# Long convolution of a hybrid encoder layer: the second DFT step on two columns at a time, with half-array matmuls and one ring of three PSUM banks

## The chip, the cores and the metric

One core of a Trainium2 chip runs the whole program. The metric is the device time of one execution in microseconds (us).

## The reference

One encoder layer is applied to two requests (256 and 2048 rows of 1024 values, all float32). An input projection gives a Hyena group (512 channels) and an attention group; both are normalised, projected and followed by a gated MLP. What this case touches is the Hyena group's long convolution, an FFT product over twice the sequence, done twice (order 2) for each request:

```python
def long_conv(z, kf, skip):
    L = z.shape[1]
    zf = z.astype(jnp.float32)
    y = jnp.fft.irfft(jnp.fft.rfft(zf, n=2 * L, axis=1) * kf[None], n=2 * L, axis=1)[:, :L]
    return (y + skip.astype(jnp.float32) * zf).astype(z.dtype)

def hyena_mixer(u, short_w, short_b, w1, b1, sin_freq, w2, b2, w3, decay, skip):
    L = u.shape[1]
    u = dwconv3(u, short_w, short_b)
    v, x1, x2 = jnp.split(u, 3, axis=-1)
    kf = hyena_filters(L, w1, b1, sin_freq, w2, b2, w3, decay)
    z = x1 * long_conv(v, kf[:, 0], skip[0])
    z = x2 * long_conv(z, kf[:, 1], skip[1])
    return z
```

The attention is a dilated sliding-window attention over 8 heads; its queries, keys and values come out of the same input projection.

## The kernel before

**The convolution in four steps.** A DFT of 2L points is split in two factors, 128 and `n2c` = 2L/128 (4 for the short request, 32 for the long one). `hyena_first` does the first factor (two matmuls `hs1`, lines 692 and 693) and stores the result in DRAM (`d_hA`). `hyena_second` works on `n2c` columns g, each a tile of 128 rows (64 real parts, 64 imaginary) by 512 channels: a float32 matmul with the table `htab` of g gives the filter's spectrum (`hs2k`, line 723), VectorE scales it (`hK`, line 725), a second matmul gives the signal's spectrum (`hs2z`, line 727), VectorE makes the four partial products of the complex product in four instructions on 64 partitions each (lines 731 to 734), GpSimd adds them (line 735), and one column later a matmul takes the product back (`hs3`, line 741; its tile is called `hs` in the trace), ScalarE copies it to `hbe` (line 744), and a DMA stores two columns in `d_hB`. The last step, in `hyena`, loads `hD` from `d_hB`, does two matmuls that use 64 of the array's columns each (`hs4`, line 778), multiplies with the gate (line 779) and either feeds `hyena_first` again (order 0) or stores to `d_hy` (order 1). There are 36 columns in each order, 72 in all, so 36 pairs of columns.

**PSUM and rings.** The pool `h_ps` has three banks: two in turn for `hs2k` and `hs2z` (tag `hps`), one for `hs1`, `hs3` and `hs4` (tag `hpt`). SBUF tiles of two columns come from the ring `hr` (4 buffers), `hk` has one buffer.

**What runs beside it.** `weave` runs generators in turn: at each step it takes the stream whose count of steps is smallest against its rate. In the first part the convolution (rate 135) runs beside the second half of the input projection, query, key and value columns (matmuls `pj`, transposes `pjt`); in the second part (rate 90) beside the attention (rate 440; scores `aS`, transposes `aT`, values `aOp`). Each `yield` is a step. Before, `hyena_second` has a yield after each column's products and one after each column's `hs3`: four for a pair of columns; the whole convolution has 216 steps. From the order in which the program is written, the framework's scheduler makes an order of instructions for each engine; each engine then runs its own in that order. When both streams have ended, the output projection (`om`, with transposes `ot`) goes through 9 chunks of 256 rows; the first chunk is the short request, and every later chunk needs rows of `d_hy` that the long request's last `hs4` steps write.

The choice of the next stream is this:

```python
            x = min(live, key=lambda y: (y[2] + 0.5) / y[1])
            x[2] += 1
```

Of the kernel before, what the change touches and what calls it, by code (L numbers as in the profile page):

```python
# [21 lines left out]
P = 128  # L22
# [26 lines left out]
def _dft(L):  # L49
# [34 lines left out]
    ti = np.transpose(t, (0, 2, 1))  # L84
# [105 lines left out]
class Hybrid:  # L190
# [488 lines left out]
    def hyena_first(self, wp, psp, r, An, n, z):  # L679
# [3 lines left out]
        for k in range(2):  # L683
# [6 lines left out]
            for h in range(2):  # L690
                ps = psp.tile([P, C], F32, tag="hpt", name="hs1", bufs=1)
# [6 lines left out]
    def hyena_second(self, wp, psp, r, o, A, B):  # L698
# [10 lines left out]
        be = None  # L709
        for g in range(n2c + 1):  # L710
            cur = None
            if g < n2c:
                i = g % 2
                if i == 0:
                    gs = slice(g, g + 2)
                    tab = wp.tile([P, 2, 2, P], F32, tag="htab", name="htab", bufs=2)
                    nc.sync.dma_start(out=tab, in_=self.a[f"tab_{r}"][:, gs])
                    xz = self.ring(wp, "hx")
                    nc.sync.dma_start(out=xz, in_=Ag[:, gs])
                    xk = wp.tile([P, 2, C], F32, tag="hk", name="hk", bufs=1)  # L720
                    nc.sync.dma_start(out=xk, in_=Kg[:, gs])
# [16 lines left out]
            if prev is not None:  # L738
# [3 lines left out]
                if g2 % 2 == 0:  # L742
                    be = self.ring(wp, "hbe")
                nc.scalar.copy(be[:, g2 % 2], ps)
                if g2 % 2 == 1:
                    nc.sync.dma_start(out=Bg[:, g2 - 1:g2 + 1], in_=be)
# [939 lines left out]
```

## Time and profile before

| | us |
|---|---|
| median of 3 executions | 3562.38 (3561.86 to 3563.61) |
| the profiled execution | 3565.03 |
| its span in the trace | 3562.9 |
| TensorE busy | 3303.1 (93%) |
| VectorE busy | 2465.5 (69%) |
| ScalarE busy | 1561.9 (44%) |
| GpSimd busy | 1255.2 (35%) |
| granted TensorE clock, mean | 0.957 |

The profiled execution took 2.1 us more than its span in the trace shows, and 2.7 us more than the median. In the trace a matmul's end is modelled and matmuls overlap, so TensorE's throughput is read from the distance between the starts of successive instructions, not from their durations. A float32 matmul of the program stands in the trace as two instructions.

### The profile page before, as it was taken

The numbers are of one execution on the slowest core, as the hardware profiler recorded it, in microseconds if no ns is written. First come the engines' busy times: TensorE is split into PE (matmuls) and PEld (weight loads), VectorE is DVE, ScalarE is ACT, GpSimd is POOL, SyncE is SP. The second block draws the span as 40 slices with busy tenths as digits, with TensorE's granted clock in tenths as the row PEclk, the third lists the DMA queues.
The fourth block names the chain that finished last, engine by engine and source line by source line (L and its number), as shares of the span: only waits on it lengthen the run. The fifth ranks groups of instructions, "written<-read, shape, count | busy, mean of one in ns | idle before, by whom it ended". The sixth has DMA issues, their size and how long they took to land.

```text
span 3562.9 us, 56859 instructions
## 1 busy us (share of the span) xinstructions
PE 3303.1 (93%) x20926; PEld 3020.3 (85%) x20926; DVE 2465.5 (69%) x4254; ACT 1561.9 (44%) x2926; POOL 1255.2 (35%) x946
## 2 busy tenths in 40 slices
PE   7989899999899999996588799999899999899998
PEld 4978798889677788773388799999899999899998
DVE  7898877764576564686388666766776666567657
ACT  4577753323345565541255433333433334344433
POOL 1487751124222231222144433333634333223222
PEclk9999999999989999997699899999999999999999
DMA  6453567676756585656666632444544224466655
GB/s 240 134 179 122 154 186 240 225 223 199 202 173 194 149 235 157 187 176 195 212 188 199 198 108 106 153 154 151 218 147 150 95 94 147 155 205 217 221 179 181
DMA packets 408334, 628.02 MB, mean 176 GB/s; under 512 B 28431, under 2 KB 231439, under 8 KB 402135
## 3 DMA queue, kind: packets, MB, share of 16 engines
q1 hardware_dynamic: 354896, 593.13, 51.2%
q10 hardware_dynamic: 52072, 28.40, 2.7%
q8 instruction: 166, 2.72, 0.3%
q0 software_dynamic: 1088, 2.85, 0.2%
q14 instruction: 112, 0.92, 0.1%
HBM read 419.03 MB, written 205.25 MB: 175 GB/s over the span
## 4 chain that ended last, share of the span: by engine, by line
PE 58%; DVE 7%; DMA 7%; issue 2%; ACT 2%; SPq 1%; POOL 1%; ACTq 0%; DVEq 0%; POOLq 0%
PE w L210 8%; PE w L208 8%; PE w L209 8%; PE fd L210 4%; PE fd L209 4%; PE fd L208 4%; PE aOp L938 4%; PE aS L906 2%; PE aS L907 2%; PE aT L922 2%; PE hs2k L723 1%; PE hs2z L727 1%; PE hs L741 1%; PE pj L209 1%; PE pj L208 1%
## 5 line engine op out<-in xcount | busy, mean ns | idle before, releaser
L208 PE MATMUL w<-hh,whi 128*128 128x288 f32 (+1 forms) x2464 | 735.4, 299 | 16.3 <-ACT whi L1345 9.9
L210 PE MATMUL w<-hh,wlo 128*128 128x290 f32 (+1 forms) x2464 | 732.2, 298 | 10.7 <-POOL wlo L203 7.0
L209 PE MATMUL w<-hl,whi 128*128 128x288 f32 (+1 forms) x2464 | 735.2, 299 | 5.2 <-DVE hl L203 5.1
L208 PEld LDWEIGHTS w<-hh,whi 128*128 128x128 f32 x2464 | 470.3, 191 | 18.2 <-ACT whi L1345 10.1
L210 PEld LDWEIGHTS w<-hh,wlo 128*128 128x128 f32 x2464 | 469.4, 191 | 12.7 <-POOL wlo L203 8.0
L209 PEld LDWEIGHTS w<-hl,whi 128*128 128x128 f32 x2464 | 472.0, 192 | 6.7 <-DVE hl L203 6.6
L208 PE MATMUL pj<-hThi,wihi 128*128 128x386 f32 (+1 forms) x1152 | 402.5, 350 | 6.6 <-ACT u L629 4.1
L209 PE MATMUL pj<-hTlo,wihi 128*128 128x386 f32 (+1 forms) x1152 | 400.9, 348 | 7.8 <-DVE hTlo L203 7.8
L210 PE MATMUL pj<-hThi,wilo 128*128 128x386 f32 (+1 forms) x1152 | 397.8, 345 | 0.0
L208 PE MATMUL fd<-hh,dwh 128*128 128x288 f32 x1210 | 359.9, 297 | 12.6 <-ACT dwh L1551 12.6
L210 PE MATMUL fd<-hh,dwl 128*128 128x288 f32 x1210 | 358.8, 297 | 0.0
L209 PE MATMUL fd<-hl,dwh 128*128 128x288 f32 x1210 | 357.5, 295 | 0.0
L735 POOL TENSOR_TENSOR ht<-ht,ht 128x512 f32<-128x512 f32 x72 | 99.0, 1376 | 432.3 <-DVE ht L734 364.1
L208 PEld LDWEIGHTS fd<-hh,dwh 128*128 128x128 f32 x1210 | 229.8, 190 | 13.3 <-ACT dwh L1551 12.9
L209 PEld LDWEIGHTS pj<-hTlo,wihi 128*128 128x128 f32 x1152 | 221.8, 193 | 20.7 <-DVE hTlo L203 9.7
L938 PEld LDWEIGHTS aOp<-aV,aPT 128*128 128x128 f32 (+1 forms) x1408 | 193.9, 196 | 52.5 <-issue 20.3
L208 PEld LDWEIGHTS pj<-hThi,wihi 128*128 128x128 f32 x1152 | 221.1, 192 | 17.7 <-ACT u L629 4.4
L210 PEld LDWEIGHTS pj<-hThi,wilo 128*128 128x128 f32 x1152 | 220.9, 192 | 12.2 <-issue 8.0
L209 PEld LDWEIGHTS fd<-hl,dwh 128*128 128x128 f32 x1210 | 229.3, 190 | 0.4
L210 PEld LDWEIGHTS fd<-hh,dwl 128*128 128x128 f32 x1210 | 227.6, 188 | 0.1
L203 POOL TENSOR_TENSOR wlo<-ws,whi 128x512 fp32r<-128x512 f32 x88 | 133.4, 1516 | 235.9 <-ACT whi L1345 235.9
L910 DVE CUSTOM_DVE_ANT_0 aP<-aS,aB 128x256 f32<-128x256 f32 (+2 forms) x432 | 136.2, 355 | 115.6 <-PE aS L907 43.4
(297 smaller groups left out, 7977.3 us busy)
## 6 DMA issues: line engine op xcount, KB each, us to landing
hl<-d_G SPq DMA_DIRECT2D x154, 288.0 KB, 5.3
dwl<-d_S SPq DMA_DIRECT2D x59, 704.0 KB, 4.1
wiraw<-in_w_in SPq DMA_DIRECT2D x72, 512.0 KB, 4.6
d_G<-cv SPq DMA_DIRECT2D x42, 576.0 KB, 3.0
wraw<-in_w_gate SPq DMA_DIRECT2D x22, 1024.0 KB, 4.8
wraw<-in_w_up SPq DMA_DIRECT2D x22, 1024.0 KB, 5.6
adat<-in_ada_t SPq DMA_DIRECT2D x36, 512.0 KB, 4.6
d_fA<-fae SPq DMA_DIRECT2D x72, 256.0 KB, 3.1
```

The source lines that it names most:

```text
L203: eng.tensor_tensor(out=lo, in0=x, in1=hi.bitcast(F32), op=ALU.subtract)
L208: mm(out, wh, xh, start=first, stop=False, skip_group_check=more)
L209: mm(out, wh, xl, start=False, stop=False, skip_group_check=more)
L210: mm(out, wl, xh, start=False, stop=last, skip_group_check=more)
L723: nc.tensor.matmul(ps, tab[:, i, 0], xk[:, i], start=True, stop=True)
L727: nc.tensor.matmul(ps, tab[:, i, 0], xz[:, i], start=True, stop=True)
L735: nc.gpsimd.tensor_tensor(out=t1, in0=t1, in1=t2, op=ALU.add)
L906: nc.tensor.matmul(ps[:, hh, :N], qa, rhs, start=True, stop=False)
L907: nc.tensor.matmul(ps[:, hh, :N], qb, rhs, start=False, stop=True)
L910: nc.vector.tensor_tensor_reduce(out=sb[:, hh, :n], in0=ps[:, hh, v0:v0 + n], in1=bias[:, hh, b0:b0 + n], scale=1.0, scalar=3e38, op0=ALU. ...
L922: nc.tensor.transpose(pt[:cn, hh, c], sb[:, hh, c0:c0 + cn], self.ident)
L938: nc.tensor.matmul(po[:, i, hs], pe[:cn, hh, c], vt[:cn, x["v"] + c * x["vs"], hs], start=(c == 0), stop=(c == len(ch) - 1))
```

## The change

The table of the inverse step is laid out anew on the host, so that its rows of the real parts of two columns stand together, and those of the imaginary parts.

`hyena_second` now takes a pair of columns in each round. A helper `forward` fills one PSUM bank with the real parts of both columns (j = 0) or with the imaginary parts of both (j = 1), by two matmuls that use all 128 rows and 64 columns of the array each; one writes partitions 0 to 63, the other 64 to 127. So real and imaginary parts stand in banks of their own, on the same partitions, and the complex product takes four VectorE instructions on 128 partitions for a pair of columns, where it took eight on 64 partitions; the two scalings and the two additions on GpSimd for a pair stay. The way back is four matmuls for a pair, each with 64 rows and 128 columns of the array: for j = 0 and j = 1 one for each column, and each column has its own bank. `hs1`, `hs2k`, `hs2z`, `hs3` and `hs4` all draw on one tag (`hp`) with three banks in turn. The SBUF tiles of the product share one tag with six buffers, as many as the three tags before had together. A pair of columns has three yields (after the scalings, after the products, after the way back), where it had four; the whole convolution has 180 steps.

```diff
-    ti = np.transpose(t, (0, 2, 1))
+    ti = np.transpose(t, (0, 2, 1)).reshape(n2c // 2, 2, 2, 64, 128).transpose(0, 2, 1, 3, 4).reshape(n2c, 128, 128)
...
-                ps = psp.tile([P, C], F32, tag="hpt", name="hs1", bufs=1)
+                ps = psp.tile([P, C], F32, tag="hp", name="hs1")
...
-        for g in range(n2c + 1):
+        halves = (slice(0, 64), slice(64, 128))
+        v = nc.vector
+
+        def forward(x, j, name):
+
+            ps = psp.tile([P, C], F32, tag="hp", name=name)
+            for i, rows in enumerate(halves):
+                nc.tensor.matmul(ps[rows], tab[:, i, 0, 64 * j:64 * j + 64], x[:, i], start=True, stop=True)
+            return ps
+
+        for g in range(0, n2c + 2, 2):
...
-                ps = psp.tile([P, C], F32, tag="hps", name="hs2k")
-                nc.tensor.matmul(ps, tab[:, i, 0], xk[:, i], start=True, stop=True)
-                K = wp.tile([P, C], F32, tag="hK", name="hK", bufs=2)
-                nc.vector.tensor_tensor(out=K, in0=ps, in1=rnc, op=ALU.mult)
-                ps = psp.tile([P, C], F32, tag="hps", name="hs2z")
-                nc.tensor.matmul(ps, tab[:, i, 0], xz[:, i], start=True, stop=True)
-                t1 = wp.tile([P, C], F32, tag="ht1", name="ht1", bufs=3)
-                t2 = wp.tile([P, C], F32, tag="ht2", name="ht2", bufs=1)
-                v, lo_, up = nc.vector, slice(0, 64), slice(64, 128)
-                v.tensor_tensor(out=t1[lo_], in0=ps[lo_], in1=K[lo_], op=ALU.mult)
-                v.tensor_tensor(out=t1[up], in0=ps[lo_], in1=K[up], op=ALU.mult)
-                v.scalar_tensor_tensor(out=t2[lo_], in0=ps[up], scalar=-1.0, in1=K[up], op0=ALU.mult, op1=ALU.mult)
-                v.tensor_tensor(out=t2[up], in0=ps[up], in1=K[lo_], op=ALU.mult)
-                nc.gpsimd.tensor_tensor(out=t1, in0=t1, in1=t2, op=ALU.add)
-                cur = (g, tab, t1)
+                K = []
+                for j in range(2):
+                    ps = forward(xk, j, "hs2k")
+                    K.append(wp.tile([P, C], F32, tag="ht", name="hK", bufs=6))
+                    v.tensor_tensor(out=K[j], in0=ps, in1=rnc, op=ALU.mult)
+                yield
+                pp = []
+                ps = forward(xz, 0, "hs2z")
+                for j in range(2):
+                    pp.append(wp.tile([P, C], F32, tag="ht", name="ht", bufs=6))
+                    v.tensor_tensor(out=pp[j], in0=ps, in1=K[j], op=ALU.mult)
+                ps = forward(xz, 1, "hs2z")
+                for j, op in ((1, ALU.subtract), (0, ALU.add)):
+                    v.tensor_tensor(out=K[j], in0=ps, in1=K[j], op=ALU.mult)
+                    nc.gpsimd.tensor_tensor(out=pp[1 - j], in0=pp[1 - j], in1=K[j], op=op)
+                cur = (g, tab, pp)
                 yield
             if prev is not None:
                 g2, tb, pp = prev
-                ps = psp.tile([P, C], F32, tag="hpt", name="hs3", bufs=1)
-                nc.tensor.matmul(ps, tb[:, g2 % 2, 1], pp, start=True, stop=True)
...
+                be = self.ring(wp, "hbe")
+                ps = [psp.tile([P, C], F32, tag="hp", name="hs3") for _ in range(2)]
+                for j in range(2):
+                    for i, rows in enumerate(halves):
+                        nc.tensor.matmul(ps[i], tb[rows, j, 1], pp[j][rows], start=(j == 0), stop=(j == 1))
+                for i in range(2):
+                    nc.scalar.copy(be[:, i], ps[i])
+                nc.sync.dma_start(out=Bg[:, g2:g2 + 2], in_=be)
                 yield
...
-                    ps = psp.tile([P, C], F32, tag="hpt", name="hs4", bufs=1)
+                    ps = psp.tile([P, C], F32, tag="hp", name="hs4")
...
-        psH = self.pool(hy, "h_ps", bufs=2, space=PSUM, side="left")
+        psH = self.pool(hy, "h_ps", bufs=3, space=PSUM, side="left")
```

The change also moves instructions against the streams beside them. Three places on TensorE show it, in the order in which its instructions stand.

At the end of the attention, before: the last two of the steps `hs4` (`hs`, line 778) of 16 in a row, with no attention work left beside them; then the second output chunk's transposes and matmuls.

```order
L778 MATMUL hs_14454<-hD,hgi_5119 64x512 x2
L778 MATMUL hs_14512<-hD,hgi_5119 64x512 x2
L1174 MATMUL ot<-ident,ohy 128x128 x4
L1174 MATMUL ot<-ident,oat 128x128 x4
L1174 MATMUL ot<-ident,ohy 128x128 x4
L1174 MATMUL ot<-ident,oat 128x128 x4
L208 MATMUL om<-omh,ow 128x256 x3
```

The same place now: the last score matmuls, transposes and value products, and right behind them the first output chunk; no `hs` stands here.

```order
L916 MATMUL aS<-Ks,Ql 128x256
L931 MATMUL aT<-ident,aP 128x128 x3
L947 MATMUL aOp<-aV,aPT 128x65 x2
L931 MATMUL aT<-ident,aP 128x128 x4
L947 MATMUL aOp<-aV,aPT 128x65 x6
L1183 MATMUL ot<-ident,ohy 128x128 x4
L1183 MATMUL ot<-ident,oat 128x128 x4
```

Inside the attention now, the last step `hs4` of the program: it stands behind 732 of the 864 score matmuls.

```order
L915 MATMUL aS<-Ks,Qh 128x192
L916 MATMUL aS<-Ks,Ql 128x192
L787 MATMUL hs_12520<-hD,hgi_5119 64x512 x2
L947 MATMUL aOp<-aV,aPT 128x65 x4
L931 MATMUL aT<-ident,aP 128x128 x2
```

The last 16 `hs4` steps moved from behind the attention to between its blocks, and the output projection moved up to the attention's end.

At the start of the attention, before: parts of columns of the long request's first order stand among the last projection transposes (`pjt`).

```order
L601 MATMUL pjt<-ident,u 128x128 x6
L727 MATMUL hs2z<-hx,htab 128x512
L723 MATMUL hs2k<-hk,htab 128x512
L601 MATMUL pjt<-ident,u 128x128 x3
L741 MATMUL hs_6671<-ht_6647,htab 128x512
L601 MATMUL pjt<-ident,u 128x128 x3
L741 MATMUL hs_6731<-ht_6664,htab 128x512
L906 MATMUL aS<-Ks,Qh 128x192
```

The same place now. The shape printed is that of the result: `64x512 x2` is one pair of half-column matmuls, and two rows `hs` of `128x512 x2` are the way back of one pair of columns.

```order
L601 MATMUL pjt<-ident,u 128x128 x6
L716 MATMUL hs2k<-hk,htab 64x512 x4
L716 MATMUL hs2z<-hx,htab 64x512 x2
L601 MATMUL pjt<-ident,u 128x128 x6
L716 MATMUL hs2z<-hx,htab 64x512 x2
L752 MATMUL hs_7849<-ht,htab 128x512 x2
L752 MATMUL hs_7850<-ht,htab 128x512 x2
L915 MATMUL aS<-Ks,Qh 128x192
```

What moved: where single whole-array matmuls of neighbouring columns stood one by one, the half-array matmuls of a whole pair of columns stand in three groups. By count over the whole order, 12 columns of `hs2z` and of `hs3` stood ahead of the first score matmul, and 38 and 36 do now; 48 and 47 stood between the first and the last score matmul, and 34 and 36 do now; 12 and 13 stood behind it, and none does now. Of the 36 steps `hs4`, 4 stood ahead of the attention, 16 in it and 16 behind it; now 4 and 32. TensorE's visits to this work (groups of `hs2k`, `hs2z`, `hs3` and `hs4` that stand together, with other work ahead and behind) number 154 up to the last score matmul before, of which 20 are `hs4` steps alone; now they number 158, and in 24 of them `hs2` or `hs4` and `hs3` stand together.

## Rows read from the trace of the kernel before

**Rows 1.** The first lines of the page: busy time of TensorE, its weight loads, VectorE and GpSimd over the whole execution, and TensorE's granted clock in 40 equal slices of the span (tenths of full speed).

```profile
PE 3303.1 (93%) x20926; PEld 3020.3 (85%) x20926; DVE 2465.5 (69%) x4254; ACT 1561.9 (44%) x2926; POOL 1255.2 (35%) x946
...
PEclk9999999999989999997699899999999999999999
```

**Rows 2.** Busy time of each engine in five stretches that follow each other (us from the span's start; in brackets how many instructions; then the granted clock of TensorE, the DMA engines' mean busy share and what they moved). The first is the second half of the input projection, the second runs from the first to the last score matmul of the attention, the third and fourth lie between that and the second chunk of the output projection, the fifth is the rest of the output projection.

```profile
534.00:944.30 410.30, 381.43 (x1984) 348.99 (x1983) 257.08 (x360) 125.63 (x200) 93.08 (x56) 0.97 0.67 214
944.30:1585.50 641.20, 617.07 (x3376) 495.97 (x3375) 424.36 (x1341) 343.09 (x823) 165.28 (x126) 0.96 0.63 185
1585.50:1675.00 89.50, 67.29 (x301) 41.77 (x298) 67.47 (x115) 22.21 (x40) 28.71 (x24) 0.89 0.60 189
1675.00:1754.30 79.30, 35.32 (x80) 7.90 (x80) 15.54 (x22) 5.55 (x13) 1.75 (x1) 0.50 0.75 239
1754.30:2000.00 245.70, 213.40 (x1664) 207.85 (x1662) 189.54 (x383) 129.41 (x276) 100.22 (x95) 0.93 0.63 193
```

**Rows 3.** TensorE's timeline around the last score matmul (`aS`), at the first output matmul (`om`), and two output matmuls later on. Columns: start us, duration us, engine, line, operation, out<-in, shapes, count.

```profile
1585.08 0.42 PE L907 MATMUL aS<-Ks,Ql 128*128 128x256 f32 x1
...
1600.47 0.48 PE L208 MATMUL om<-omh,ow 128*128 128x256 f32 x2
...
1640.56 0.28 PE L210 MATMUL om<-omh,owl 128*128 128x256 f32 x1
1640.68 0.28 PE L208 MATMUL om<-omh,owh 128*128 128x256 f32 x1
```

**Rows 4.** The chain of work that ended last, in order of time, between the attention and the second output chunk: start us, us, what.

```profile
1681.38 1.99 PE hs L778 x4
...
1695.45 5.56 DMA d_hy<-hg
...
1703.54 5.28 DMA d_hy<-hg
...
1742.71 2.64 DMA ohy<-d_hy
...
1754.52 1.26 PE om L208 x5
```

**Rows 5.** TensorE's groups by line and shape in the first stretch (534 to 944.3): the long convolution's. Two instructions of the trace make one matmul of the program. After the count: busy us, mean ns of one | idle time of the engine just before them, and who ended most of it.

```profile
L692 PE MATMUL hs<-hS,hf 128*128 128x512 f32 x40 | 16.8, 419 | 9.1 <-DVE hae L694 8.3 <-ACT hae L694 0.8
L727 PE MATMUL hs2z<-hx,htab 128*128 128x512 f32 x24 | 13.5, 644 | 6.8 <-DMA hx<-d_hA 4.6 <-issue 1.3 <-DVE ht L734 0.9
```

**Rows 6.** The same in the second stretch (944.3 to 1585.5).

```profile
L727 PE MATMUL hs2z<-hx,htab 128*128 128x512 f32 x96 | 55.2, 659 | 5.9 <-DVE ht L734 5.4 <-DMA hx<-d_hA 0.5
L741 PE MATMUL hs<-ht,htab 128*128 128x512 f32 x96 | 53.5, 640 | 4.8 <-POOL ht L735 4.8
L778 PE MATMUL hs<-hD,hgi 128*64 128x512 f32 x64 | 17.3, 617 | 0.6 <-DMA hD<-d_hB 0.6
```

**Rows 7.** The same in the third and fourth stretch together (1585.5 to 1754.3).

```profile
L778 PE MATMUL hs<-hD,hgi 128*64 128x512 f32 x64 | 31.6, 1087 | 32.9 <-DVE hg L779 25.2 <-DMA hD<-d_hB 7.7
L741 PE MATMUL hs<-ht,htab 128*128 128x512 f32 x26 | 15.8, 692 | 8.8 <-POOL ht L735 8.8
L727 PE MATMUL hs2z<-hx,htab 128*128 128x512 f32 x24 | 13.7, 653 | 8.8 <-DVE ht L734 4.4 <-DMA hx<-d_hA 4.4
L723 PE MATMUL hs2k<-hk,htab 128*128 128x512 f32 x22 | 13.1, 682 | 2.5 <-DMA htab<-in_tab 2.5
```

**Rows 8.** TensorE's timeline: two whole-array float32 matmuls of the program behind each other (each two instructions, x2).

```profile
1646.32 1.02 PE L727 MATMUL hs2z<-hx,htab 128*128 128x512 f32 x2
1647.17 1.02 PE L723 MATMUL hs2k<-hk,htab 128*128 128x512 f32 x2
```

**Rows 9.** TensorE's timeline around one step `hs4` (line 778), whose two matmuls use half of the array's columns each (four instructions, x4), and around a block of transposes without one ahead of it (first two rows).

```profile
1335.56 0.65 PE L922 MATMUL aT<-ident,aP 128*128 128x128 f32 x4
1335.97 0.52 PE L906 MATMUL aS<-Ks,Qh 128*128 128x192 f32 x1
...
1336.54 0.41 PE L906 MATMUL aS<-Ks,Qh 128*128 128x192 f32 x1
1336.77 0.41 PE L907 MATMUL aS<-Ks,Ql 128*128 128x192 f32 x1
1337.12 1.08 PE L778 MATMUL hs<-hD,hgi 128*64 128x512 f32 x4
1338.13 0.66 PE L922 MATMUL aT<-ident,aP 128*128 128x128 f32 x4
1338.54 0.58 PE L906 MATMUL aS<-Ks,Qh 128*128 128x256 f32 x1
```

**Rows 10.** TensorE's timeline early in the program: the filter MLP's matmuls. Line 359 gives rows 0 to 63 of the array to one product and rows 64 to 127 to another, each with 64 columns; line 354 uses rows 0 to 32, with the lower or the upper 64 columns. "64*64" is rows*columns of the array that one instruction uses.

```profile
60.80 0.54 PE L359 MATMUL mlp<-h,w 64*64 64x384 f32 x2
60.82 0.53 PE L354 MATMUL mlp<-ft,w 33*64 33x384 f32 x1
61.17 0.49 PE L359 MATMUL mlp<-h,w 64*64 64x384 f32 x2
```

**Rows 11.** The second DFT step's elementwise work over the whole execution, by line and shape (columns as in rows 5).

```profile
L725 DVE TENSOR_TENSOR hK<-hs2k,hrn 128x512 f32<-128x512 f32 x72 | 49.7, 691 | 10.8 <-PE hs2k L723 9.0
L731 DVE TENSOR_TENSOR ht<-hs2z,hK 64x512 f32<-64x512 f32 x72 | 48.9, 678 | 41.8 <-PE hs2z L727 41.3
```

**Rows 12.** The longest piece of its kind in the chain that ended last: the load of the filter's columns (`hk`, one buffer).

```profile
985.45 7.58 DMA hk<-d_fA
```

More of the change, by code (lines that the diff above doesn't have):

```diff
@@ L708, in hyena_second @@
         prev = None
-        be = None
-        for g in range(n2c + 1):
+        halves = (slice(0, 64), slice(64, 128))
[6 more added lines that the diff above has]
+        for g in range(0, n2c + 2, 2):
             cur = None
             if g < n2c:
[L713 to L721, printed above, removed]
-                ps = psp.tile([P, C], F32, tag="hps", name="hs2k")
-                nc.tensor.matmul(ps, tab[:, i, 0], xk[:, i], start=True, stop=True)
-                K = wp.tile([P, C], F32, tag="hK", name="hK", bufs=2)
-                nc.vector.tensor_tensor(out=K, in0=ps, in1=rnc, op=ALU.mult)
-                ps = psp.tile([P, C], F32, tag="hps", name="hs2z")
-                nc.tensor.matmul(ps, tab[:, i, 0], xz[:, i], start=True, stop=True)
-                t1 = wp.tile([P, C], F32, tag="ht1", name="ht1", bufs=3)
-                t2 = wp.tile([P, C], F32, tag="ht2", name="ht2", bufs=1)
-                v, lo_, up = nc.vector, slice(0, 64), slice(64, 128)
-                v.tensor_tensor(out=t1[lo_], in0=ps[lo_], in1=K[lo_], op=ALU.mult)
-                v.tensor_tensor(out=t1[up], in0=ps[lo_], in1=K[up], op=ALU.mult)
-                v.scalar_tensor_tensor(out=t2[lo_], in0=ps[up], scalar=-1.0, in1=K[up], op0=ALU.mult, op1=ALU.mult)
-                v.tensor_tensor(out=t2[up], in0=ps[up], in1=K[lo_], op=ALU.mult)
-                nc.gpsimd.tensor_tensor(out=t1, in0=t1, in1=t2, op=ALU.add)
-                cur = (g, tab, t1)
@@ new lines, in hyena_second @@
+                gs = slice(g, g + 2)
+                tab = wp.tile([P, 2, 2, P], F32, tag="htab", name="htab", bufs=2)
+                nc.sync.dma_start(out=tab, in_=self.a[f"tab_{r}"][:, gs])
+                xz = self.ring(wp, "hx")
+                nc.sync.dma_start(out=xz, in_=Ag[:, gs])
+                xk = wp.tile([P, 2, C], F32, tag="hk", name="hk", bufs=1)
+                nc.sync.dma_start(out=xk, in_=Kg[:, gs])
+                K = []
[3 more added lines that the diff above has]
+                    v.tensor_tensor(out=K[j], in0=ps, in1=rnc, op=ALU.mult)
@@ L739, in hyena_second @@
                 g2, tb, pp = prev
-                ps = psp.tile([P, C], F32, tag="hpt", name="hs3", bufs=1)
-                nc.tensor.matmul(ps, tb[:, g2 % 2, 1], pp, start=True, stop=True)
[L742 to L746, printed above, removed]
+                be = self.ring(wp, "hbe")
[6 more added lines that the diff above has]
+                nc.sync.dma_start(out=Bg[:, g2:g2 + 2], in_=be)
                 yield
```

## The prediction

> **What bounds the kernel now.** I read the page's first lines, then the engines by stretch, then the chain between the attention and the output projection. TensorE is busy for 93% of the span and VectorE for 69% [rows 1]; that is an average over stages with different limits. In the second half of the input projection TensorE is busy 381.4 of 410.3 us, in the attention 617.1 of 641.2 us [rows 2]: TensorE is the bound there, and whatever is added to its queue shows. Behind the last score matmul (1585.08) it is not. The second chunk of output matmuls starts at 1754.5 [rows 3, 4], and in the last 79 us of these 169 us TensorE is busy for 35 us and at half its clock, 0.50 granted, the 1.2 GHz level [rows 2]. The chain says why: `hs4` steps of the long request, each behind the last one's store or load, DMAs of 5 us [rows 4], with nothing else to run. The convolution runs out after the attention does. I call these 169 us the tail.
>
> **The change part by part.** Two whole-array float32 matmuls stand 0.85 us apart [rows 8], so one instruction of a whole-array float32 matmul costs 0.425 us in a stream. An `hs4` step, which is two matmuls on half the columns each, took 1.01 us from its start to the next instruction's [rows 9]. So two column halves run at the same time, and a pair costs about what one whole matmul does. The new `hs2k` and `hs2z` have that very form (128 rows, 64 columns, 512 wide): a pair of columns needs four such pairs of halves in place of four whole matmuls, no more stream time.
>
> The way back is four matmuls of 64 rows and 128 columns in place of two whole ones. That form is not in the trace. If two row halves run together it costs nothing; if not, 72 pairs of halves cost 0.85 us more each, 61 us. The nearest rows are the filter MLP's: line 359 has a product on rows 64 to 127 and the upper columns in flight when line 354, 20 ns later, starts one on rows 0 to 32 [rows 10]; the lower columns of those rows were taken by line 359's other product, so the two shared columns and differed in rows. I take nothing.
>
> *The tail, -124.* By the order printed above no convolution work stands behind the attention. What is left of 168.8 us (1754.3 less 1585.5): to the first output matmul 10 us, where it took 15.4 with convolution columns in between [rows 3]; 192 output matmuls of the first chunk at 0.12 us, 23 us [rows 3]; the next chunk's 16 transposes at 0.1 us (four take 0.41 [rows 9]), 2 us; and 10 us for weight loads and splits that no longer lie under the convolution. Together 45 us. With no wait it is 35, with twice as much 65.
>
> *Work that moves into stretches where TensorE is the bound, +45.* From the tail, 26, 24 and 22 instructions of `hs3`, `hs2z` and `hs2k` [rows 7] at 0.425 are 31 us, 16 `hs4` steps at 0.85 are 14 us. Were it all to fall into TensorE's idle time in the two stretches, 29 + 24 = 53 us [rows 2], it would cost nothing; that time is spread over short waits, so I take it whole. Where among the two it lands (25 more columns in the projection, 12 fewer in the attention) doesn't change the sum.
>
> *Going into and out of half-array matmuls, +45.* A visit to `hs4` costs more than its stream: 1.01 against 0.85, and the score matmul ahead of it holds TensorE for 0.35 us (1336.77 to 1337.12) where the one before held it 0.23 [rows 9]; the transposes behind it take 0.41 us to the next score matmul, as those without an `hs4` ahead do [rows 9]. That is 0.28, say 0.3 us for a visit. There were 20 such visits up to the last score matmul, now all 158 are: 138 × 0.3 = 41 us, and 24 visits in which column halves meet row halves add 0.15 each, 4 us. The lower end is 138 × 0.16 = 22 us. The upper: `hs4` is busy 17.3 us in 16 visits, 1.08 each [rows 6], which with the 0.12 ahead is 0.35 over the stream, 48 us and 4. A rule speaks for this term too: the Trainium skill, "TensorEngine Tiling (Array Packing)", Key Properties under Tiling Modes, says that a change of tiling mode, not of the tile alone, drains the engine. By it every entry and exit would show a whole run-out; a pair of whole matmuls is busy 1.02 us and streams in 0.85 [rows 8], so 0.17 us at each of 300 more changes (two a visit and the 24, less 40 before) is 51 us in place of 45, and the forecast 6 us later. The trace agrees on entry and inside the visit, not behind it.
>
> *VectorE, banks, loads, -1.* A pair of columns took two scalings and eight products, 0.69 us each, though the products had 64 partitions [rows 11]; now six instructions on 128 partitions do, at the same 0.69 as the scaling shows: 2.8 us less for a pair, 99 us of VectorE's time in all. It isn't the bound, so this pays only where TensorE waits for it. In the attention `hs2z` waited 5.4 us for the products' bank and `hs3` 4.8 us for the sum behind them [rows 6]; I take half, -5. In the projection `hs1` waited 8.3 us for its one bank [rows 5]; with three in turn I take -8. Against it stand the loads: in the projection TensorE waited 4.6 us for `hx` in six pairs [rows 5], 1 us a pair with the smaller ones; the projection now holds 12.5 more pairs, +12. The ends: no gain, or all 53 us of idle time; and for the loads nothing, or the 7.6 us that a load of `hk` held the chain [rows 12] for each of the 12.5 pairs, 95 us. The new yields need no term of their own: what they do is the order shown above.
>
> The sum is -124 + 45 + 45 - 1 = -35 us. The profiled execution took 3565.0, 2.7 over the median of 3562.4; from the median I get 3527 us.
>
> **The rivals.** *Row halves one after the other.* The way back then costs 61 us more: 3588. It decides from the point where 57% of these halves are serial (35 of 61). For it: no row shows 64 rows with 128 columns twice at once. Against it: the MLP's products, and that each of the two has its own bank.
>
> *The projection waits for loads.* `hk` has one buffer, so a pair's load starts when the pair before is done with it; behind a waiting `hs2k` stand the projection's matmuls. At 7.6 us for each of 12.5 pairs the time is 3610; it is slower from 3.8 us a pair. Against it: 1 us a pair so far, and a DMA share of 0.67 in that stretch [rows 2].
>
> *The wait moves with the work.* If the 16 `hs4` steps hold TensorE in the attention as they did behind it (32.9 us idle [rows 7]), the time is 3560, no change to measure. Against it: 16 steps in the attention waited 0.6 us in all [rows 6].
>
> *More relief.* If a VectorE with 99 us less to do takes most of TensorE's idle 53 us away, and with it the stretches of half clock (0.97 and 0.96 granted [rows 2]), the time is 3485.
>
> **How the numbers follow.** My forecast 0.52 (its own range 3505 to 3550), more relief 0.18, serial row halves 0.13, loads 0.09, the moved wait 0.08. A change of 0.2%, 7 us, is what a measurement of this kernel can tell from none. Faster: 0.52 + 0.18 = 0.70. Same: 0.08. Slower: 0.13 + 0.09 = 0.22. The range that holds 8 in 10 runs from 3475, below more relief, to 3590, the serial row halves; it leaves out the dear loads and the ends of the others.
>
> **What would show it.** In the new profile: no stretch at a granted 0.50 between attention and output, and the second output chunk about 45 us behind the last score matmul (the tail); first and second stretch together longer by some 90 us (moved work and visits), the first by most of it; two instructions of the way back starting within 20 ns of each other (row halves); 1.0 us from the start of a pair of halves to the next instruction outside, and not 0.86 (visits); VectorE busy 99 us less. The prediction is wrong if row halves start 0.43 us apart, if `hk` or `hx` end TensorE's idle time in the projection by tens of us, or if the tail keeps more than 80 us.

## The result

The changed kernel takes 3592.84 us (median of 5 runs, 3580.66 to 3601.96), the kernel before 3563.61 us beside it; the ratio is 1.0082, 95% interval 1.0057 to 1.0107. It is slower by 0.8%, where 1% faster was forecast, and the time lies 3 us above the range.

The first lines of the page of the changed kernel answer to [rows 1].

```profile
PE 3389.1 (94%) x21358; PEld 3014.4 (84%) x21358; DVE 2349.8 (65%) x4110; ACT 1562.1 (44%) x2922; POOL 1265.8 (35%) x946
...
PEclk9999999999999989899699999999999999999999
```

VectorE has 116 us less to do. TensorE has 86 us more. Where the tail had two slices of the granted clock at 7 and 6 tenths, one at 6 is left (the twentieth, 1706 to 1795; it holds a piece of the attention too, see the last section).

Busy time by stretch, the same columns as in [rows 2]: from the convolution's first matmul to the first score matmul, from there to the last, from there to the 193rd output matmul, and 230 us of the rest of the output projection. Before, the 193rd output matmul opened the second output chunk, so the third row is what the third and fourth of [rows 2] are together. In the changed order the second chunk opens with the 97th, 48.7 us behind the last score matmul, and its first matmuls stand among the last of the first chunk.

```profile
534.60:1059.80 525.20, 499.89 (x2359) 367.00 (x2357) 293.81 (x410) 138.76 (x221) 121.76 (x79) 0.99 0.64 208
1059.80:1745.20 685.40, 663.49 (x3565) 498.75 (x3564) 329.57 (x1220) 337.85 (x809) 152.54 (x115) 0.92 0.61 178
1745.20:1805.40 60.20, 38.23 (x247) 35.48 (x246) 38.06 (x92) 28.12 (x55) 16.40 (x14) 0.69 0.56 168
1805.40:2035.00 229.60, 203.66 (x1666) 199.56 (x1664) 179.63 (x356) 120.57 (x264) 111.17 (x95) 0.99 0.69 210
```

The tail fell from 168.8 to 60.2 us, as it was meant to. Behind it another 23 us are saved (1754.3 to the end were 1808.6 us, 1805.4 to the end are 1785.6). The first stretch grew by 115 us and the second by 44, and TensorE is busy for nearly all of that: 118 and 46 us more. So the time was not lost in waits. TensorE has more to do. Which line does it shows in TensorE's groups over the whole execution (line, shape, count of instructions | busy us, mean ns | idle before, releaser).

```profile
L752 PE MATMUL hs<-ht,htab 64*128 64x512 f32 x288 | 136.8, 618 | 0.0
L716 PE MATMUL hs2z<-hx,htab 128*64 128x512 f32 x288 | 79.8, 642 | 3.4 <-DVE wilo L203 3.4
L716 PE MATMUL hs2k<-hk,htab 128*64 128x512 f32 x288 | 79.6, 671 | 7.8 <-DMA htab<-in_tab 7.8
```

All three lines hold 288 instructions on half the array. The column halves (line 716) are busy for 80 us each, what the whole matmuls of before took. The row halves (line 752) are busy for 137 us. The timeline of the changed kernel shows both forms: first a group of four row halves alone, then a group of four column halves with row halves behind them.

```profile
1315.70 0.54 PE L916 MATMUL aS<-Ks,Ql 128*128 128x192 f32 x1
1316.18 1.98 PE L752 MATMUL hs<-ht,htab 64*128 64x512 f32 x4
1318.09 1.09 PE L931 MATMUL aT<-ident,aP 128*128 128x128 f32 x4
...
1335.27 1.08 PE L716 MATMUL hs2z<-hx,htab 128*64 128x512 f32 x4
1336.28 2.09 PE L752 MATMUL hs<-ht,htab 64*128 64x512 f32 x6
1338.10 0.33 PE L947 MATMUL aOp<-aV,aPT 64*128 64x65 f32 x2
1338.21 1.02 PE L752 MATMUL hs<-ht,htab 64*128 64x512 f32 x2
1339.16 0.55 PE L915 MATMUL aS<-Ks,Qh 128*128 128x192 f32 x1
```

Four instructions of column halves, a pair of matmuls, took 1.01 us from their start to the next instruction (1335.27 to 1336.28), as [rows 9] had it. Four of row halves took 1.91 us (1316.18 to 1318.09): one after the other. But at 1336.28 eight of them, with a product of the attention between, went through in 2.9 us to the next score matmul at 1339.16, less than eight one after the other would need (3.4 at 0.43). So some row halves do overlap. The order of the instructions tells which. The four at 1316.18 are two matmuls of one column: both on the same 64 rows, both into the same bank, the first for j = 0 and the second for j = 1. That is what the order printed ahead of the prediction holds too: `hs_7849 ... x2`, then `hs_7850 ... x2`, each row one bank. The program writes j = 0 for both columns and then j = 1; the scheduler sent both matmuls of one bank first. Rows and bank go together in this program, so no run tells which of the two keeps them apart. Of the 144 matmuls of the way back 66 are followed by the other one on the same rows, 6 by one on the other rows, and 72 by different work.

### The profile page after: what moved, and what is told of

Read it like the earlier page. It is cut to its first block, busy times and chain, and to the rows that moved or that the text cites. A ratio compares the mean times of both kernels' runs of the same rounds, so it can differ in the third digit from the quotient of the medians.

```text
span 3591.0 us, 57575 instructions
## 1 busy us (share of the span) xinstructions
PE 3389.1 (94%) x21358; PEld 3014.4 (84%) x21358; DVE 2349.8 (65%) x4110; ACT 1562.1 (44%) x2922; POOL 1265.8 (35%) x946
## 4 chain that ended last, share of the span: by engine, by line
PE 40%; DVE 5%; issue 2%; DMA 2%; ACT 1%; POOL 1%; SPq 0%; ACTq 0%; DVEq 0%; POOLq 0%
PE w L210 9%; PE w L208 9%; PE w L209 9%; PE fd L210 4%; PE fd L209 4%; PE fd L208 4%; DVE fT L1260 0%; DMA d_x1T<-ox 0%; DVE hl L203 0%; DVE ohy L1168 0%; DMA hl<-d_opT 0%; POOL oat L1154 0%; DVE ox L1223 0%; PE om L208 0%; PE om L210 0%
## 5 line engine op out<-in xcount | busy, mean ns | idle before, releaser
L947 PEld LDWEIGHTS aOp<-aV,aPT 128*128 128x128 f32 (+1 forms) x1408 | 204.6, 209 | 51.8 <-issue 19.1
L743 POOL TENSOR_TENSOR ht<-ht,hK 128x512 f32<-128x512 f32 x72 | 95.8, 1352 | 400.9 <-DVE hK L742 375.0
L947 PE MATMUL aOp<-aV,aPT 128*128 128x65 f32 (+1 forms) x1408 | 223.3, 296 | 8.3 <-ACT aPT L935 4.5
```

Of the source, the lines that this page charges most:

```text
L743: nc.gpsimd.tensor_tensor(out=pp[1 - j], in0=pp[1 - j], in1=K[j], op=op)
L947: nc.tensor.matmul(po[:, i, hs], pe[:cn, hh, c], vt[:cn, x["v"] + c * x["vs"], hs], start=(c == 0), stop=(c == len(ch) - 1))
```

## Experiments

Two theories stood against each other. By the first, row halves run together, and only their order in TensorE's queue kept them apart. By the second, row halves of 128 columns don't run together. Then the other parts of the change were taken one by one.

**Row halves side by side.** The four matmuls of a pair are held together in turns of rows, and the first waits for the last product of the spectrum's first bank (`free`), so that two banks are there.

```diff
-                for j in range(2):
-                    for i, rows in enumerate(halves):
-                        nc.tensor.matmul(ps[i], tb[rows, j, 1], pp[j][rows], start=(j == 0), stop=(j == 1))
+                last = None
+                for j in range(2):
+                    for i in (1, 0):
+                        mm = nc.tensor.matmul(ps[i], tb[halves[i], j, 1], pp[j][halves[i]], start=(j == 0), stop=(j == 1))
+                        if last is not None:
+                            self.tc.keep_in_program_order(mm)
+                        elif cur is not None:
+                            self.tc.add_manual_dep(mm.ins, free.ins.name, mybir.DependencyInfo(
+                                mybir.DependencyClass.Sync, mybir.DependencyReason.DATA), reason="both banks")
+                        last = mm
```

> The changed kernel with one thing added: the four half matmuls of a pair's way back are held together in TensorE's queue (upper rows, lower rows, upper rows, lower rows), the first of them waiting for both banks. In the changed kernel the two that stand next to each other are the two of the same rows and bank, 0.43 us apart. Theory 1, row halves run together and only the order in the queue kept them apart: the way back falls from 137 us busy to about 75 us, the time from 3593 to about 3533 us, and instructions on the two row halves start within 20 ns of each other. Theory 2, row halves of 128 columns do not run together whatever the order: 3593 us within 7, starts still 0.43 us apart. Theory 3, they run together but holding them behind both banks costs what it gains: starts within 20 ns, time above 3570 us.

Measured: 3546.37 us, ratio to before 0.9958 (0.9945 to 0.9972), 46 us under the changed kernel and 13 over the first theory's 3533. Its first two stretches, then two rows of TensorE's timeline in the attention and the group of the way back (now line 753) over the whole execution:

```profile
536.30:1025.90 489.60, 463.36 (x2309) 357.76 (x2308) 282.77 (x399) 135.37 (x218) 112.68 (x77) 0.98 0.66 216
1025.90:1695.80 669.90, 638.47 (x3613) 480.00 (x3612) 346.17 (x1234) 338.18 (x810) 151.47 (x118) 0.95 0.63 188
```

```profile
1299.84 1.99 PE L753 MATMUL hs<-ht,htab 64*128 64x512 f32 x8
1301.76 0.63 PE L938 MATMUL aT<-ident,aP 128*64 128x128 f32 x4
```

```profile
L753 PE MATMUL hs<-ht,htab 64*128 64x512 f32 x288 | 76.2, 617 | 0.9 <-DVE ht L739 0.7 <-ACT hbe L761 0.2
```

In the order 104 of the 144 matmuls are now followed by one on the other rows, and none by one on the same. It takes the wait for the second bank: in the scheduler's order without that wait (a version that was not timed), the first of the four still stands by itself, some instructions ahead of the other three. Eight instructions now take the time that four took, and in the trace their starts stand in couples 7 ns apart (1299.844 and 1299.851, 1300.378 and 1300.385, and so on). The line's busy time fell from 136.8 to 76.2 us. Theory 2 has fallen. The Trainium skill, "TensorEngine Tiling (Array Packing)", Key Properties, says that tiles operate independently and that different ones can execute in parallel; this row agrees, and the row at 1316.18 adds that two instructions of one tile, into one bank, don't. Of the 61 us less busy, 46 came back as time. In the first two stretches TensorE is busy 62 us less (1163.4 to 1101.8) and idle 10 us more (47.2 to 57.7). What this idle time waits for I didn't separate.

**The way back whole.** GpSimd's last add and subtract write real and imaginary part of a column under each other, and the way back is two whole matmuls again, with the table of before. The products keep four of their six buffers, and the sums get two.

```diff
-                    nc.gpsimd.tensor_tensor(out=pp[1 - j], in0=pp[1 - j], in1=K[j], op=op)
+                    for i, rows in enumerate(halves):
+                        nc.gpsimd.tensor_tensor(out=tt[i][halves[1 - j]], in0=pp[1 - j][rows], in1=K[j][rows], op=op)
...
-                for j in range(2):
-                    for i, rows in enumerate(halves):
-                        nc.tensor.matmul(ps[i], tb[rows, j, 1], pp[j][rows], start=(j == 0), stop=(j == 1))
+                for i in range(2):
+                    nc.tensor.matmul(ps[i], tb[:, i, 1], pp[i], start=True, stop=True)
```

> The changed kernel with the way back of before: GpSimd's last add and subtract are written as four instructions on 64 partitions that put real and imaginary part of a column under each other again, and two whole-array matmuls with the table of before take the place of four on 64 rows. Both theories of the row halves say the same of it: 62 us of serial stream and some 20 us of going into and out of the row halves (72 pairs by 0.3) are gone, 3511 us. It gives the price of the row-half form whole: against it the adjacent order shows what the visits cost when the halves do run together. If GpSimd's longer sum (four instructions of about 1.5 us in place of two of 1.35) is waited for, the way back waits on it in the attention and the time stays above 3560 us.

Measured: 3521.37 us, ratio 0.9897 (0.9881 to 0.9914): 71 us under the changed kernel, 10 short of the 82 expected, and 25 us under the row halves side by side. The way back itself is as long in both:

```profile
L753 PE MATMUL hs<-hq,htab 128*128 128x512 f32 x144 | 76.7, 616 | 1.0 <-POOL hq L745 1.0
```

So row halves that run together cost no stream, as forecast, but the form costs 25 us in what stands around it: TensorE is busy 27 us less in the first two stretches without it (1075.3 against 1101.8; the profiled execution, 3514.8 us, was the fastest of its six). With row halves side by side the order has 40 groups of row halves, and 178 visits to half-array matmuls against 114 here: 0.6 us each by the first count, 0.4 for each of the 64 visits more by the second. How much of it is the form and how much the wait for two banks I didn't separate.

**The pace alone.** The kernel before, with the convolution's rate raised.

```diff
-    RATES = dict(p1=42, f=90, ad=36, h1=135, p2=39, h2=90, at=440)
+    RATES = dict(p1=42, f=90, ad=36, h1=162, p2=39, h2=108, at=440)
```

> The kernel before, with nothing of the change but the convolution's pace: its share of turns is raised by 1.2 in both stages (135 to 162 and 90 to 108), the ratio in which the change has fewer turns for the same work. Theory: the tail behind the attention went because the turns became fewer, not because of half matmuls. Then the stretch from the last score matmul to the second output chunk falls from 169 to about 60 us, the two stretches before it grow by the moved work alone, about 45 us, and the time is 3562 - 109 + 45 = 3500 us, 60 us under the changed kernel even with its halves mended to 3533. Rival: the pace is limited by the products on VectorE or by loads, so that a faster pace only makes TensorE wait in the attention: the tail goes, the first two stretches grow by 100 us or more, 3550 to 3565 us.

Measured: 3560.68 us, ratio 0.9998 (0.9989 to 1.0007). Neither theory: nothing moved. The stretches are 407.0, 638.4 and 177.2 us, and 13 columns of `hs2z` and 12 of `hs2k` still stand behind the attention.

**Pace and banks; the banks alone; the banks otherwise.** In the kernel before, all four steps take one tag with three banks in turn, once with the higher rate and once without. The third version keeps two tags and divides the three banks the other way round, one for `hs2k` and `hs2z`, two for `hs1`, `hs3` and `hs4`.

```diff
-                ps = psp.tile([P, C], F32, tag="hpt", name="hs1", bufs=1)
+                ps = psp.tile([P, C], F32, tag="hp", name="hs1")
...
-        psH = self.pool(hy, "h_ps", bufs=2, space=PSUM, side="left")
+        psH = self.pool(hy, "h_ps", bufs=3, space=PSUM, side="left")
```

> The kernel before with the faster pace of the run before it and the shared ring of three banks, whole matmuls throughout. Theory: the banks give TensorE back the 8 us that the first step waited for its one bank in the projection and some 5 us of waits in the attention, 10 us under the run with the pace alone, about 3490 us. Rival: these waits are taken over by others and the banks are worth nothing, the same within 5 us.

> The kernel before with the three banks alone: all four steps of the convolution take them in turn in place of two banks for the second step's forward products and one for the three others; whole matmuls, the pace of before. Theory 1, the one bank that the first step, the way back and the last step shared held the convolution back into the tail, and the pace has nothing to do with it: the same as with pace and banks, 3492 us within 6, second output chunk 37 us behind the last score matmul. Theory 2, the banks and the pace are both needed: the tail keeps over 100 us, 3540 to 3560 us.

> The kernel before with its three banks divided the other way: one for the second step's forward products and two for the first step, the way back and the last step. Theory 1, what held the convolution back was a bank that nobody else could use while it stood idle, so it is the sharing of all three and not the number for one kind: no gain, 18 columns forward are left behind the attention in the order (11 before), the tail is some 10 to 15 us longer than the 169 before, 3565 to 3585 us. Theory 2, the one bank for the three other steps was the hold: the tail goes, below 3520 us.

Measured: pace and banks 3491.79 us, 0.9808 (0.9792 to 0.9825); the banks alone 3487.51 us, 0.9788 (0.9765 to 0.9811); the banks otherwise 3623.79 us, 1.0163 (1.0130 to 1.0196). Pace and banks came out as expected, though the pace alone had brought nothing; the banks alone as in the first theory. The banks otherwise gained nothing, as its first theory had it, but lie 39 us over that theory's upper end. (The 37 us of the expectation for the banks alone count to the 49th output matmul. The second chunk opens 45.6 us behind the last score matmul there, and the 193rd output matmul stands at 57, where the stretch below ends.) The three stretches of the banks alone, and of the banks divided 1 to 2:

```profile
535.80:987.60 451.80, 423.84 (x2077) 365.81 (x2077) 315.82 (x437) 134.40 (x214) 119.04 (x72) 0.98 0.69 224
987.60:1636.30 648.70, 621.13 (x3414) 489.52 (x3412) 417.20 (x1336) 338.96 (x814) 156.10 (x122) 0.96 0.68 200
1636.30:1693.40 57.10, 36.21 (x246) 34.13 (x245) 38.56 (x93) 28.36 (x57) 19.16 (x16) 0.73 0.61 180
```

```profile
537.10:953.40 416.30, 391.49 (x2004) 352.53 (x2003) 265.22 (x372) 126.49 (x202) 90.78 (x58) 0.98 0.65 213
953.40:1579.30 625.90, 597.77 (x3309) 488.65 (x3308) 382.67 (x1293) 338.61 (x814) 151.46 (x118) 0.94 0.61 178
1579.30:1827.30 248.00, 143.14 (x427) 65.31 (x425) 108.58 (x174) 32.39 (x62) 41.23 (x32) 0.72 0.54 170
```

The banks alone take the whole tail away, with whole matmuls and the old pace. In the order, 29 columns of `hs2k` stand ahead of the attention (13 before) and none behind it (11 before); with the banks divided 1 to 2 it is 16 ahead and 18 behind, and the tail is 248 us. So a second bank for the three other steps is not what counts, and sharing all three is. I read it so: a bank that only one kind of step may use lies idle while the other kind waits, and the scheduler's order follows what is free, where the rates order only the program's text. That the pace did nothing fits this; no row shows it directly. The kernel with the banks alone beats both, the one before by 2.1% and the changed one by 2.9%.

**Two columns at a time, whole.** The changed kernel's rounds of a pair and its three turns, with the three banks, but whole matmuls and the eight products of before.

```diff
+                for i in range(2):
+                    ps = psp.tile([P, C], F32, tag="hp", name="hs2k")
+                    nc.tensor.matmul(ps, tab[:, i, 0], xk[:, i], start=True, stop=True)
...
+                ps = [psp.tile([P, C], F32, tag="hp", name="hs3") for _ in range(2)]
+                for i in range(2):
+                    nc.tensor.matmul(ps[i], tb[:, i, 1], pp[i], start=True, stop=True)
```

> The change without half-array matmuls: three banks in turn and two columns at a time with the change's order of steps and its turns, but whole matmuls with the table of before, and the products of before. Theory 1, two columns at a time is worth nothing by itself: the banks alone, 3487 us within 7, so that all the 105 us between the banks alone and the changed kernel come from the half-array form. Theory 2, two columns at a time itself costs the 15 to 25 us that visits and VectorE leave open, through bursts at which the three banks run out: 3500 to 3512 us.

Measured: 3498.73 us, ratio 0.9825 (0.9810 to 0.9841), 11 us over the banks alone; the intervals touch. Between the two expectations: taking columns in pairs costs something, at the edge of what is measured.

**Column halves alone; less VectorE alone; both.** On top of the banks alone, first each whole forward matmul as two column halves into the same bank, then two products of 128 partitions in place of four of 64, then both. The second and the third leave out that real and imaginary part meet.

```diff
-                nc.tensor.matmul(ps, tab[:, i, 0], xk[:, i], start=True, stop=True)
+                for h in range(2):
+                    nc.tensor.matmul(ps[64 * h:64 * h + 64], tab[:, i, 0, 64 * h:64 * h + 64], xk[:, i], start=True, stop=True)
```

```diff
-                v.tensor_tensor(out=t1[lo_], in0=ps[lo_], in1=K[lo_], op=ALU.mult)
-                v.tensor_tensor(out=t1[up], in0=ps[lo_], in1=K[up], op=ALU.mult)
-                v.scalar_tensor_tensor(out=t2[lo_], in0=ps[up], scalar=-1.0, in1=K[up], op0=ALU.mult, op1=ALU.mult)
-                v.tensor_tensor(out=t2[up], in0=ps[up], in1=K[lo_], op=ALU.mult)
+                v.tensor_tensor(out=t1, in0=ps, in1=K, op=ALU.mult)
+                v.tensor_tensor(out=t2, in0=ps, in1=K, op=ALU.mult)
```

> The run with the three banks alone, and each whole matmul of the second step forward (144 of them) as two column halves into the same bank: the same stream, the same products on VectorE, and 139 more visits to half-array matmuls (170 in place of 31 runs of them in TensorE's queue). Theory, a visit costs 0.3 us of TensorE's time: 42 us more than the banks alone, about 3534 us. Rival, the change of form costs only where TensorE is at the bound and streams back to back, or a visit costs less than a tenth of a us: within 10 us of the banks alone. If a visit costs what the kernel with the whole way back lost against pace and banks (30 us in 83 visits, 0.36 each), 50 us more, 3542 us.

> The run with the three banks alone, but the four products of a column on 64 partitions are left out and two on 128 partitions take their place (they multiply the wrong halves; this leaves out that real and imaginary part meet): VectorE has 2.8 us less for a pair of columns, as much as the change saves, and nothing else moves. Theory, VectorE's relief is worth nothing on the path: the same as the banks alone within 7 us, 3492 us. Rival, more relief: TensorE's waits for the products shrink, 3450 to 3475 us.

> The banks alone with the two edits of the runs before it together: every whole forward matmul as two column halves (27 us dearer by itself), and two products on 128 partitions in place of four on 64 (9 us cheaper by itself; this leaves out that real and imaginary part meet). The kernel with the whole way back has both and takes 34 us more than the banks alone. Theory 1, the two add up: 18 us over the banks alone, 3506 us, and 15 us of the 34 are in something else. Theory 2, with visits in TensorE's queue the relief is worth nothing or less: 3515 to 3521 us, and the 34 us are told by the form of the matmuls.

Measured: column halves 3514.99 us, 0.9865 (0.9842 to 0.9887); less VectorE 3478.27 us, 0.9761 (0.9739 to 0.9783); both 3515.99 us, 0.9870 (0.9852 to 0.9889). The first lies between its expectations, the second 9 us under the banks alone, more than its theory and 3 us short of its rival's range, and both together as the second theory had it. The first two stretches with column halves:

```profile
537.30:1003.70 466.40, 440.29 (x2201) 351.66 (x2200) 318.72 (x441) 134.92 (x216) 115.32 (x72) 0.99 0.67 218
1003.70:1669.20 665.50, 643.28 (x3578) 478.33 (x3576) 416.10 (x1333) 336.83 (x813) 155.29 (x121) 0.96 0.67 194
```

For 139 more visits TensorE is busy 38.6 us more (1083.6 against 1045.0), 0.28 us a visit, and the kernel is 27.5 us longer, 0.20 a visit: part of it falls into TensorE's idle time (55.5 to 48.3 us in these stretches). A run-out of 0.17 at every entry and exit, as the rule weighed in the prediction would have it, would be 47 us. VectorE's relief is worth 9 us by itself and nothing beside the column halves.

**GpSimd's sum in halves.** On top of the banks alone, as many and as short instructions on GpSimd as the whole way back has.

```diff
-                nc.gpsimd.tensor_tensor(out=t1, in0=t1, in1=t2, op=ALU.add)
+                for rows in (lo_, up):
+                    nc.gpsimd.tensor_tensor(out=t1[rows], in0=t1[rows], in1=t2[rows], op=ALU.add)
```

> The banks alone, but GpSimd's sum for a column is written as two instructions on 64 partitions in place of one on 128, so that GpSimd has the four for a pair of columns that the kernel with the whole way back has. Theory 1, GpSimd's longer sum is hidden: 3487 us within 7. Theory 2, the way back waits for it: 10 to 25 us more, with TensorE's idle time before the way back up from 6 us to 15 or more.

Measured: 3490.99 us, ratio 0.9802 (0.9786 to 0.9819), 3.5 us over the banks alone and no difference that can be told. GpSimd's sum is hidden.

## Why the prediction was wrong

The versions form a staircase from the kernel before to the changed one. Each differs from the one above it by one part, the fourth by column halves with the fewer products and GpSimd's sum in halves (the stretches in us from the profiled executions, the times are medians; they were taken at four different times, with the kernel before at 3561 to 3567 us beside them):

| version | to the first score | attention | behind it | span | time |
|---|---|---|---|---|---|
| before | 410.3 | 641.2 | 1977.4 | 3562.9 | 3563 |
| + three banks in turn | 451.8 | 648.7 | 1849.3 | 3485.6 | 3487.5 |
| + two columns at a time | 450.9 | 656.6 | 1852.6 | 3496.5 | 3498.7 |
| + column halves, fewer products | 481.6 | 649.5 | 1844.9 | 3512.8 | 3521.4 |
| + row halves side by side | 489.6 | 669.9 | 1848.0 | 3543.8 | 3546.4 |
| the change: row halves as scheduled | 525.2 | 685.4 | 1845.8 | 3591.0 | 3592.8 |

*Row halves, forecast 0, measured 46 us.* This is the step that failed: "If two row halves run together it costs nothing", and then "I take nothing". The hardware does run them together where they stand side by side, and the MLP's rows [rows 10] pointed the right way (though they don't say which columns line 354's early product used, and in the program's order its first is the one on the lower columns). What failed was to go from the form of the instructions to their time without their order. The order that I had printed showed the two matmuls of one bank next to each other, and I read it only for where the work stands against the attention. The rival of serial row halves, 3588 us, came within 5 us of the result, but I had given it a chance of 0.13, for a reason of hardware that doesn't hold, and asked whether they can overlap, not whether they would. That it lies so close is in part luck: its 61 us of stream came to 46 us of time, and other terms fill the gap.

*The tail, forecast -124.* Measured -109 up to the 193rd output matmul (60.2 left, not 45; the first output matmul alone came 14 us behind the attention, not 10), and 23 us more behind it: for the same matmuls TensorE is busy 15 us less there, at a granted 0.99 in place of 0.98, and idle 8 us less. Together that is -132 behind the attention. (My ends for this term don't go together: 35 leaves out one of its two terms of 10 us, 65 doubles both.) The mechanism was right, but I left its cause open; it is the banks, which I had put at -1 with VectorE and the loads.

*Moved work, forecast +45.* The banks alone make the first two stretches 49 us longer (1051.5 to 1100.5) with the work that moved there. Right.

*Going into and out of half-array matmuls, forecast +45.* Column halves with the fewer products cost 23 us, row halves side by side 25, together 48. The sum is right, in part by luck, and its division is not: a visit to column halves costs 0.20 us of time, and one to row halves 0.4 to 0.6, by how they are counted, where I had taken the same for both.

*VectorE, banks, loads, forecast -1.* VectorE is relieved by 116 us (forecast 99) and this brings nothing beside half-array matmuls. `hk` and `hx` don't hold the projection; the longest wait for a load ahead of line 716 is 7.8 us for `htab` in all. Columns in pairs may cost 11 us, at the edge of what is measured, which the prediction didn't have.

By time, the parts are -76 (banks, with tail and moved work), +11, +23, +25 and +46; without the last one the forecast of -35 would have stood against -17. By the ratios to the kernel before they are -76, +13, +26, +22 and +44, and each ratio's interval is 5 to 9 us either way. The granted clock moved along: its mean over all executions is 0.972 with the banks alone, 0.969 with two columns at a time, 0.965 with column halves, 0.968 with row halves side by side and 0.967 with the change. By an estimate from these numbers a step of 0.003 is some 10 us in 3500 where TensorE is the bound, so the steps of 11, 23 and 25 us can hold some of it, and no run separates that. The step of 46 us hardly can.

Of the signs that the prediction named, 1.0 us for a pair of column halves came, and VectorE's relief came, larger than named. The tail's came in part: the second output chunk opens 48.7 us behind the last score matmul, but the clock was still granted at 0.50 ahead of it, while TensorE had nothing to do:

```profile
1770.00:1780.00 10.00, 0.00 (x0) 0.00 (x0) 9.35 (x12) 5.62 (x10) 6.96 (x4) 0.50 0.33 100
```

The first two stretches grew by 159 us and not by some 90. The sign against the prediction came too: row halves 0.43 us apart.

## What to carry to other kernels

Here row halves shared the array only where instructions for different rows stood next to each other in the final queue. Look up that order, and make the scheduler keep it (here by having all banks free before the first one), before counting on such an overlap. When a change bundles several edits, price the plainest one alone: three shared banks in place of two and one brought the whole gain, 76 us, and the half-array form only took from it. And a tail of work that comes late can be an allocation that keeps it from being scheduled earlier; here a higher rate didn't change that.

## What the runs showed of the hardware

Two instructions on different row halves (64 rows, 128 columns, banks of their own) start 7 ns apart and together take the time of one, 0.43 us for 512 columns of a pass. In the changed kernel two of them start 5 ns apart as well (1337.246 and 1337.251), inside the group of eight shown above.

The granted clock fell in the attention of the changed kernel to 0.92 (0.96 in [rows 2]), and I can't say from what. One piece of it lies where no convolution runs any more (its last matmul starts at 1663.0): 20 us at the 1.2 GHz level, with TensorE busy all the time before and within.

```profile
1679.80:1699.80 20.00, 20.00 (x109) 18.24 (x107) 7.06 (x35) 9.64 (x25) 0.00 (x0) 0.85 0.10 30
1699.80:1719.80 20.00, 20.00 (x87) 18.69 (x87) 4.30 (x25) 6.65 (x18) 0.00 (x0) 0.50 0.05 14
```

The kernel with the whole way back shows the same (0.50 from 1618.4 to 1638.4, its last convolution matmul at 1583.9). The banks alone, whose convolution lasts until 15 us before the attention's end, were granted 0.91 or more in the last 80 us of it. Row halves side by side, whose convolution ends 70 us before the attention does, were granted 0.70 from 1655.8 to 1675.8. No run here was made to tell whether the one brings the other.
